# A two-layer encoder in fp32 on one core: V of mixer A computed first, by seven half-sized products per head group, and the merge of each head pair emitted behind the next pair's first projection

## The chip, the cores and the metric

The kernel is one program on one core of a Trainium2 chip. The metric is the device time of one execution in microseconds (us); a kernel's time is the median of its runs. The engines are named as in the profile: PE (matrix products), PEld (its weight loads), DVE (elementwise work), ACT (activations and copies), POOL (a few small operations, and the issue of DMAs that add to what lies in the destination), SP (the issue of all other DMAs).

## The reference

A pre-norm encoder of two layers on x of shape (1, 512, 1024) in fp32. Layer 0 has mixer A, layer 1 mixer B (latent attention), and each mixer is followed by a squared-ReLU MLP of width 4096. The change touches mixer A:

```python
def dilated_mixer(h, w_qkv, q_gain, k_gain, w_o):     # h: [1, 512, 1024]
    qkv = (h @ w_qkv).reshape(B, S, 3, N_GROUPS, A_HEADS, A_HEAD_DIM)   # 3 groups, 8 heads of 128
    for g, (window, dil) in enumerate(((128, 1), (512, 4), (2048, 16))):
        q = rope(rms_norm(qkv[:, :, 0, g], q_gain[g]), S)
        k = rope(rms_norm(qkv[:, :, 1, g], k_gain[g]), S)
        v = qkv[:, :, 2, g]
        o, lse = dilated_group(q, k, v, window, dil)   # banded attention inside each residue class
        ...
    wts = softmax(stack(lses), axis=0)                 # the three groups merged by their denominators
    o = sum(wts[g][..., None] * outs[g])
    return o.reshape(B, S, A_WIDTH) @ w_o
```

So V is, for each of the three groups, one product of a 512x1024 by a 1024x1024 matrix.

## The kernel before, in words

**Products.** Every fp32 operand x is split into hi (a rounded copy, written by ACT, L157 for weights: `whi`) and lo = x - hi (DVE, L158: `wlo`), and a product is three passes, hi·hi, hi·lo and lo·hi, accumulated in a bank of PSUM. `run_block` (L161) takes a matrix in units of two 128-row slices of the weight, loads each unit from SP (`raw`), splits it, and issues its matmuls (L184) for four row tiles r, each with a bank `acc` of its own. The list `groups` says how many units are issued for a row tile before the next row tile comes: with [1, 1, 1, 1] each unit goes through all four tiles, with [4] each tile is finished in one go. `evac` empties a bank when its last unit is through. The activations hT (hi and lo) are the stationary operand, 128x128; the weights move past it, 512 or 384 columns to a matmul.

**Mixer A** runs over four pairs of heads b. A pair has three `qk_block` (L293), one to a group: 96 matmuls of 512 columns, and for each row tile an evacuation with mean squares on ACT (L136), the rotary products on DVE (L308, L311, L315, L316), transposes on PE (L123), and then scores, masks and exponentials. It has two `v_block` (L365), one to a head: 96 matmuls of 384 columns (three groups of 128), copied to `vt`; group 0's part goes to DRAM (`vd`) and comes back in another arrangement as `v0n` and `v0c`. Then `merge` (L376) weights the three groups: small matmuls that move statistics between partitions (`scm`, L386 and L411), some twenty short DVE operations, and six products of the probabilities by the weights (L417). `pv` (L419) transposes the probabilities (L123, copied out at L426) and multiplies by V (L440, L444, into `oT` at L446). In the last pair the order is V of head 0, the three `qk_block`, `merge`, V of head 1, `pv`.

**Behind it** `oT` is split into `oA` (L655, L656), and `project` (L635) multiplies by w_o in two column halves: the first in single units, the second with [4]. The MLP follows; its down projection is made in four quarters, each by seven half-sized products (`wino`, L489; matmuls L580) instead of eight, in the order of the list `ORDER` (L590). A product has its activation operand split at L485 and L486 (`asp`) and its weight at L523 and L524; sums of weights are made by DMAs from POOL that add to what lies in SBUF (L509), sums of activations on DVE (L517).

**What sets the order.** Each engine executes its instructions in one fixed row. The tile framework sets that row at build time: it simulates a timeline and places the instructions of code that is written one after the other among each other. A row of one engine can thus be read before anything runs, and the code alone does not show it.

## Time and profile before

| | |
|---|---|
| median of 3 runs | 1451.21 us (1450.21, 1451.21, 1451.93) |
| profiled execution | 1451.78 us, its span 1449.6 us, mean granted PE clock 0.999 |
| mixer A with its output projection | roughly the first 560 us of the span |
| one middle head pair (256.06 to 379.74 us) | 123.7 us |
| busy | PE 97%, PEld 83%, DVE 61%, ACT 50%, POOL 14% of the span |

Busy times of PE overstate: matmuls overlap, so the mean duration of one (some 340 to 390 ns) is longer than the time from one start to the next. The distance is read from stretches of the chain that ended last in which PE waits for nothing. The clock is 1.00 when the throttle grants full speed. An idle time in brackets in a timeline row is the time that the engine stood before that instruction, with the instruction that released it.

### The profile page before, as it was taken

How to read it: one execution, taken by the hardware profiler on the slowest of the kernel's cores; microseconds unless marked ns; L12 is line 12 of the kernel's file. 1: busy time of each engine (PE TensorE's matmuls, PEld its weight loads, DVE VectorE, ACT ScalarE, POOL GpSimd, SP SyncE). 2: the span in 40 equal slices, each digit the busy share in tenths (PEclk: the TensorE clock that was granted, in tenths of full speed). 3: DMA queues.
4: the chain of work that ended last, by engine and by line, in shares of the span. 5: the costliest groups of instructions: out<-in, count | busy, mean ns of one | idle time of the engine just before them, and what ended most of it. 6: DMA issues, size and time to landing. Idle time of an engine off the chain costs nothing.

```text
span 1449.6 us, 19315 instructions
## 1 busy us (share of the span) xinstructions
PE 1410.4 (97%) x7116; PEld 1196.8 (83%) x7116; DVE 887.1 (61%) x1421; ACT 727.2 (50%) x1590; POOL 198.4 (14%) x197
## 2 busy tenths in 40 slices
PE   7999999999999999999999999899999999999998
PEld 6889889889988878888888877776768988888877
DVE  6765566566537655266475749788755266475647
ACT  5544455355335533453544545777633454544543
POOL 1120120011011101011020222332101011020210
PEclk9999999999999999999999999999999999999999
DMA  7325114321622344749394853310013749394853
GB/s 228 100 57 162 58 49 129 110 63 45 174 92 62 97 140 141 222 112 236 91 233 127 195 136 66 99 30 30 30 44 136 206 111 239 93 223 138 189 116 88
DMA packets 134813, 177.52 MB, mean 122 GB/s; under 512 B 8768, under 2 KB 73536, under 8 KB 134720
## 3 DMA queue, kind: packets, MB, share of 16 engines
q1 hardware_dynamic: 117312, 142.74, 31.1%
q0 software_dynamic: 17408, 33.56, 14.0%
q8 instruction: 56, 0.92, 0.2%
q14 instruction: 37, 0.30, 0.1%
HBM read 172.07 MB, written 4.19 MB: 122 GB/s over the span
## 4 chain that ended last, share of the span: by engine, by line
PE 89%; ACT 4%; DVE 3%; DMA 2%; issue 1%; POOL 1%; SPq 0%; DVEq 0%; ACTq 0%; POOLq 0%
PE acc L184 58%; PE sc L580 10%; PE tp L580 7%; PE tp L123 4%; PE acc L859 1%; PE acc L835 1%; PE sc L753 1%; PE sco L444 1%; PE sco L440 1%; PE sc L351 1%; PE sc L835 1%; ACT whi L157 1%; ACT junkb L136 1%; DVE wlo L158 1%; PE tp L859 0%
## 5 line engine op out<-in xcount | busy, mean ns | idle before, releaser
L184 PE MATMUL acc<-whi,hT 128*128 128x512 f32 (+2 forms) x1600 | 486.3, 379 | 5.6 <-DVE t L311 2.2
L158 DVE TENSOR_TENSOR wlo<-raw,whi 128x1024 fp32r<-128x1024 f32 (+3 forms) x170 | 195.7, 1156 | 230.5 <-ACT whi L157 229.5
L184 PEld LDWEIGHTS acc<-whi,hT 128*128 128x128 f32 x1600 | 296.2, 189 | 47.3 <-issue 2.9
L184 PE MATMUL acc<-hT_f,whi 128*128 128x512 f32 (+1 forms) x1152 | 319.4, 366 | 1.9 <-DVE resid L641 1.2
L157 ACT ACTIVATE whi<-raw 128x1024 fp32r<-128x1024 f32 (+3 forms) x170 | 170.0, 1005 | 269.0 <-PE acc L184 177.4
L184 PE MATMUL acc<-wlo,hT 128*128 128x512 f32 (+2 forms) x800 | 300.2, 375 | 0.2 <-DVE wlo L158 0.2
L184 PEld LDWEIGHTS acc<-hT_f,whi 128*128 128x128 f32 x1152 | 208.4, 189 | 37.8 <-DVE resid L641 1.6
L524 DVE TENSOR_TENSOR wlo<-wqs,whi 128x1024 fp32r<-128x1024 f32 x112 | 137.3, 1227 | 113.6 <-ACT whi L523 113.5
L184 PE MATMUL acc<-hT_f,wlo 128*128 128x512 f32 (+1 forms) x576 | 205.1, 365 | 0.0
L523 ACT ACTIVATE whi<-wqs 128x1024 fp32r<-128x1024 f32 x112 | 118.6, 1060 | 167.6 <-PE acc L184 66.2
L184 PEld LDWEIGHTS acc<-wlo,hT 128*128 128x128 f32 x800 | 151.2, 189 | 20.5 <-DVE wlo L158 1.1
L580 PE MATMUL sc<-whi,asp 128*128 128x512 f32 x512 | 165.1, 390 | 0.8 <-ACT asp L485 0.8
L509 POOL DMA_DIRECT2D wqs<-in_ffn_w_dram x64 | 77.6, 1350 | 528.4 <-DVE wlo L524 339.9
L184 PEld LDWEIGHTS acc<-hT_f,wlo 128*128 128x128 f32 x576 | 108.6, 189 | 17.5
L131 POOL TENSOR_TENSOR qrs<-rs_v,nhalf 128x4 f32<-128x4 f32 x48 | 61.5, 1290 | 408.3 <-DVE rs_v L128 393.8
L580 PE MATMUL tp<-whi,asp 128*128 128x512 f32 x352 | 112.2, 390 | 2.6 <-DVE asp L486 2.6
L580 PEld LDWEIGHTS sc<-whi,asp 128*128 128x128 f32 x512 | 96.1, 188 | 21.6 <-ACT asp L485 1.6
L580 PE MATMUL sc<-wlo,asp 128*128 128x512 f32 x256 | 99.6, 389 | 0.0
L580 PEld LDWEIGHTS tp<-whi,asp 128*128 128x128 f32 x352 | 65.9, 188 | 17.2 <-DVE asp L486 3.5
L580 PE MATMUL tp<-wlo,asp 128*128 128x512 f32 x176 | 68.5, 389 | 0.0
L136 ACT ACTIVATE junk<-acc 128x128 f32<-128x128 f32 x192 | 53.1, 277 | 18.9 <-PE acc L184 13.8
L554 DVE TENSOR_TENSOR resid<-resid,sc 128x512 f32<-128x512 f32 x64 | 43.0, 682 | 24.4 <-PE sc L580 24.4
(190 smaller groups left out, 1796.3 us busy)
## 6 DMA issues: line engine op xcount, KB each, us to landing
wqs<-in_ffn_w_dram SPq DMA_DIRECT2D x80, 512.0 KB, 5.1
raw<-in_ffn_w_dram SPq DMA_DIRECT2D x64, 512.0 KB, 4.4
wqs<-in_ffn_w_dram POOLq DMA_DIRECT2D x64, 512.0 KB, 7.2
raw<-in_a_w_qkv_dram SPq DMA_DIRECT2D x96, 256.0 KB, 3.4
raw<-in_a_w_qkv_dram SPq DMA_DIRECT2D x64, 192.0 KB, 2.8
raw<-in_a_w_o_dram SPq DMA_DIRECT2D x8, 512.0 KB, 4.0
raw<-in_b_w_o_dram SPq DMA_DIRECT2D x8, 512.0 KB, 3.7
xt<-in_x_dram SPq DMA_DIRECT2D x8, 256.0 KB, 5.7
```

The lines of the kernel that those rows point to most:

```text
L123: PE.transpose(o, i, ident)
L131: G.tensor_tensor(out, v[:, :n], nhalf[:, :n], op=ALU.pow)
L136: A.activation(junk, x, AF.Square, scale=1.0 / math.sqrt(dim), accum_out=out)
L157: A.activation(hi[:, :nk, :n], raw[:, :nk, :n], AF.Copy)
L158: V.tensor_tensor(lo[:, :nk, :n], raw[:, :nk, :n], hi[:, :nk, :n].bitcast(F32), op=ALU.subtract)
L184: PE.matmul(accs[o][:, oc], lhsT=lt, rhs=rt, start=(kt == 0 and p_i == 0 and hv == 0), stop=(kt == total - 1 and p_i == 2), skip_group_che ...
L509: nc.gpsimd.dma_start(t, src, accum_op=ALU.add)
L523: A.activation(hi, x, AF.Copy)
L524: V.tensor_tensor(lo, x, hi.bitcast(F32), op=ALU.subtract)
L554: V.tensor_tensor(sl, sl, banks[t], op=op)
L580: PE.matmul(bk[t], lhsT=lt, rhs=rt[:, j], start=(first and k == 0 and i_ == 0), stop=(k == 3 and i_ == 2), skip_group_check=True)
L835: PE.matmul(sc, lhsT=lt, rhs=rt, start=(i == 0), stop=(i == 4))
```

## The change

1. **V phase.** `v_phase` computes V of all heads before the pairs. For each group the 512x1024 by 1024x1024 product is cut into 2x2 blocks and made by seven products of half size in each dimension, 24 matmuls of 512 columns each, instead of eight. The sums of activations that the products need (`Ssp`, from copies `h32` and `stg` of the transposed rows) are made once, on DVE. Of the sums of weights one is added on DVE (`sum1`, `bT`), one on DVE (`b3`), and two are made by adding DMAs from POOL (`add_block`, 2 of 512 KB each). Banks are emptied by `put` into `vo`, and V goes to DRAM (`vall`). The Q and K projection of pair 0, group 0 is made inside this phase, by code of its own, ahead of the products. The v_block of before, their loads and their copies are gone.
2. **Pairs.** `v_load` reads a pair's V back from DRAM. The Q and K projections use groups [2, 2] instead of [1, 1, 1, 1]. `scores` and the projection of the next group alternate, and `finish` (merge and pv) of pair b is emitted behind the first projection of pair b+1.
3. **Last pair.** `oA` is split for heads 0 to 5, and the first three of the four units of the output projection's first column half (they need only heads 0 to 5) are emitted ahead of `finish`; the fourth unit follows the last `pv`.
4. **Last down projection** of each MLP: `ORDER_LAST` moves product 2 ahead of products 5 and 3.

The diff, cut to its core:

```diff
-    def run_block(units, groups, n, mm, evac, outs=NT, name=None, halves=1):
+    def block_groups(units, groups, n, mm, outs=NT, halves=1):
...
-                        evac(o, accs[o])
+                        yield o, accs[o]
             kt0 = nkt
+            if gi < len(groups) - 1:
+                yield None
...
+    def qk_proj(b, g, qkT, homes, junk):
+        run_block(qk_units(b, g), [2, 2], 512, act_stationary(hT, 512),
+                  lambda r, acc: qk_evac(g, qkT, r, acc, homes, junk)())
...
+        def add_block(t, g, ki, ni):
+            for u in range(2):
+                nc.gpsimd.dma_start(t[:, 2 * u:2 * u + 2], wblk(g, ki, ni, u), accum_op=ALU.add)
...
+        def sum1(g, u):
+            us = slice(2 * u, 2 * u + 2)
+            V.tensor_tensor(bT[g][:, us], b11[g][:, us], b12[g][:, us], op=ALU.add)
...
+        def piece(g, ba, bd, parts):
+            put(g, 0, 0, "set", ba, False)
+            put(g, 0, 0, "add", bd, True)
+            bb = new_banks("b")
+            both(5, bT[g], bb, True, parts)
+            put(g, 1, 1, "set", bb, False)
+            add_block(bT[g], g, 1, 1)
+            both(3, b22[g], bb, False, parts)
+            put(g, 0, 1, "set", bb, False)
+            b3 = vp.tile([P, 4, 512], F32, tag="h32", name=nm("b3"))
+            for u in range(2):
+                us = slice(2 * u, 2 * u + 2)
+                V.tensor_tensor(b3[:, us], b12[g][:, us], b22[g][:, us], op=ALU.add)
+            both(6, bT[g], ba, False, parts)
+            put(g, 0, 1, "sub", ba, True)
+            add_block(bT[g], g, 1, 0)
+            both(7, b3, ba, False, parts)
+            put(g, 1, 1, "sub", ba, True)
+            both(4, bT[g], ba, False, parts)
+            put(g, 1, 0, "set", ba, True)
...
+        for g in range(1, NG):
+            fetch(g)
+            parts = {}
+            ba, bd = new_banks("a"), new_banks("d")
+            both(1, b11[g], ba, True, parts)
+            both(2, b21[g], bd, True, parts)
+            for u in range(2):
+                sum1(g, u)
+            piece(g, ba, bd, parts)
...
-            if last:
-                vs = [v_all(0)]
-                qk_all()
-                merge(stats, Pt, True)
-                vs.append(v_all(1))
-                oA = new_hT()
-            else:
-                qk_all()
-                vs = [v_all(0), v_all(1)]
-                merge(stats, Pt, False)
-            for h in range(2):
-                pv(b, h, Pt, *vs[h])
+            vs = v_load(b)
+            for g in range(NG):
+                scores(b, g, qkT, Pt, stats)
+                if g + 1 < NG:
+                    qkT = project_in(b, g + 1)
+            if b + 1 < HA // 2:
+                qkT = project_in(b + 1, 0)
+                finish(b, Pt, stats, vs)
+        oA = new_hT()
...
+        for h in range(HA - 2):
+            split_o(h)
+        first_cols = block_groups(w_units(a_w_o[0], 0, 512), [3, 1], 512, act_stationary(oA, 512))
+        next(first_cols)
+        finish(HA // 2 - 1, Pt, stats, vs)
+        for h in (HA - 2, HA - 1):
+            split_o(h)
...
-        for p, chain, first, (i, n, op) in ORDER:
+        for p, chain, first, (i, n, op) in ORDER if done is None else ORDER_LAST:
...
+    ORDER_LAST = [ORDER[0], ORDER[4]] + ORDER[1:4] + ORDER[5:]
```

Three places show what this does to the rows of the engines.

DVE's row at the start of mixer A, before: `cosg` and `sing` are the rotary tables, `hT` the lo part of the last row tile, `t` the rotary products of the first two banks.

```order
L289 TENSOR_TENSOR cosg_104<-ca,gqk 128x4x128
L291 TENSOR_TENSOR sing_107<-ca,gqk 128x4x128
L289 TENSOR_TENSOR cosg_104<-ca,gqk 128x4x128
L291 TENSOR_TENSOR sing_107<-ca,gqk 128x4x128
L221 TENSOR_TENSOR hT_91<-tp_212,hT_91 128x4x128
L221 TENSOR_TENSOR hT_91<-tp_219,hT_91 128x4x128
L308 TENSOR_TENSOR t_59_296<-acc_243,cosg_104 128x512
L311 TENSOR_TENSOR t_60_297<-acc_243,sing_107 128x4x64 x2
```

The same stretch of DVE's row now, from the lo part of the last row tile to the first split of a V weight (`bT` is a sum of weight blocks, `Ssp` and `stg` belong to the sums of activations, `wlo_408` is the lo part of the first V weight):

```order
L408 TENSOR_TENSOR stg_241<-stg_241,h_109 128x512
L362 TENSOR_TENSOR hT_91<-tp_257,hT_91 128x4x128
L362 TENSOR_TENSOR hT_91<-tp_262,hT_91 128x4x128
L272 TENSOR_TENSOR t_51_382<-acc_141,cosg_103 128x512
L272 TENSOR_TENSOR t_55_399<-acc_142,cosg_103 128x512
L275 TENSOR_TENSOR t_51_382<-acc_141,sing_104 128x4x64 x2
L275 TENSOR_TENSOR t_55_399<-acc_142,sing_104 128x4x64 x2
L448 TENSOR_TENSOR bT_158<-b_11_146,b_13_152 128x1024 x2
L128 TENSOR_SCALAR rs_v_522<-qss_513 128x4
L384 TENSOR_TENSOR Ssp_115<-stg_241,Ssp_115 128x4x128
L372 TENSOR_TENSOR stg_271<-h_109,stg_271 128x512
L422 TENSOR_TENSOR wlo_408<-b_11_146,whi_407 128x1024
```

The four table operations still stand right ahead of these rows; sums of weights and of activations have come in between the rotary products and the next split of a weight.

PE's row around the last pair's merge, before: `acc_4717` is the last bank of V of head 1, `sc` the last group's scores, `acc_4987` and on the banks of the output projection's first column half, `scm` the merge's small matmuls.

```order
L184 MATMUL acc_4717<-wlo_4815,hT_91 128x384
L184 MATMUL acc_4717<-whi_4814,hT_91 128x384
L351 MATMUL sc_4654<-qkT_4433 128x128
L351 MATMUL sc_4666<-qkT_4433 128x128
L351 MATMUL sc_4654<-qkT_4433 128x128
L351 MATMUL sc_4666<-qkT_4433 128x128
L184 MATMUL acc_4987<-whi_4993,hT_4858 128x512
L184 MATMUL acc_4987<-wlo_4994,hT_4858 128x512
L184 MATMUL acc_4988<-whi_4993,hT_4858 128x512
L184 MATMUL acc_4988<-wlo_4994,hT_4858 128x512
```

Behind these come, before, the merge's first small matmuls, some 60 matmuls of the output projection, and its second small matmuls. The same place in PE's row now (`acc_4589` is the last of the output projection's four banks, with the third of its units, `whi_4604`, at the end):

```order
L183 MATMUL acc_4589<-wlo_4599,hT_4573 128x512
L183 MATMUL acc_4589<-whi_4598,hT_4573 128x512
L592 MATMUL sc_4549<-qkT_4328 128x128
L592 MATMUL sc_4561<-qkT_4328 128x128
L183 MATMUL acc_4589<-whi_4604,hT_4573 128x512
L183 MATMUL acc_4589<-wlo_4605,hT_4573 128x512
L183 MATMUL acc_4589<-whi_4604,hT_4573 128x512 x2
L183 MATMUL acc_4589<-wlo_4605,hT_4573 128x512
L183 MATMUL acc_4589<-whi_4604,hT_4573 128x512
L630 MATMUL scm_4683<-ca,xsel_4680 128x4 x4
L655 MATMUL scm_4704<-ca,xsel_4680 128x4 x2
L123 MATMUL tp_4714<-ck,P_4022 128x128 x4
```

The output projection's 72 matmuls stand ahead of and among the last scores, six of them behind; between the merge's two small steps and the transposes stands nothing else.

DVE's row at the start of the last down projection, before (`wlo` are weight splits, `S` sums of activations, `asp` the lo parts of activations, `resid` the results):

```order
L524 TENSOR_TENSOR wlo_12129<-wqs_10046,whi_12128 128x1024
L524 TENSOR_TENSOR wlo_12145<-wqs_10046,whi_12144 128x1024
L517 TENSOR_TENSOR S_12121<-a_2046_11516 128x1024
L517 TENSOR_TENSOR S_12162<-S_12121,a_2046_11516 128x1024
L524 TENSOR_TENSOR wlo_12169<-wqs_10046,whi_12168 128x1024
L554 TENSOR_TENSOR resid<-resid,sc_12085 128x512
L486 TENSOR_TENSOR asp_12123<-S_12121,asp_12123 128x4x256
```

And now:

```order
L784 TENSOR_TENSOR wlo_11878<-wqs_9795,whi_11877 128x1024
L784 TENSOR_TENSOR wlo_11894<-wqs_9795,whi_11893 128x1024
L777 TENSOR_TENSOR S_11913<-a_2007_11265 128x1024
L746 TENSOR_TENSOR asp_11872<-a_2007_11265,asp_11872 128x4x256
L777 TENSOR_TENSOR S_11954<-S_11913,a_2007_11265 128x1024
L814 TENSOR_TENSOR resid<-resid,sc_11834 128x512
L784 TENSOR_TENSOR wlo_11921<-wqs_9795,whi_11920 128x1024
L746 TENSOR_TENSOR asp_11915<-S_11913,asp_11915 128x4x256
```

The second product's operand no longer is a sum; the sum's lo part (`asp_11915`) stands one product later in PE's use.

## The prediction

> **What bounds the kernel now.** The page's head and its summary of the chain that ended last come first.

> ```profile
> span 1449.6 us, 19315 instructions
> PE 1410.4 (97%) x7116; PEld 1196.8 (83%) x7116; DVE 887.1 (61%) x1421; ACT 727.2 (50%) x1590; POOL 198.4 (14%) x197
> PE 89%; ACT 4%; DVE 3%; DMA 2%; issue 1%; POOL 1%; SPq 0%; DVEq 0%; ACTq 0%; POOLq 0%
> ```

> PE is the bound, and the other engines release it seldom. So matmuls removed count in full wherever PE stays fed, and the price of one must be a distance from start to start. I take it from two stretches of the chain in which PE waits for nothing, the first of 512 columns, the second (the two v_block of a pair) of 384; the three rows behind show a middle pair's merge.

> ```profile
> 29.36 9.80 PE acc L184 x43
> 362.57 17.17 PE acc L184 x99
> ...
> 256.06 0.79 PE scm L386 x8
> 256.85 8.08 PE acc L184 x35
> 264.93 0.34 PE scm L411 x4
> ```

> 9.80/43 = 0.2279 us for 512 columns, 17.17/99 = 0.1734 us for 384. In the merge, 35 matmuls of other work already stand between its two steps. The table by windows (us, then busy time of PE, PEld, DVE, ACT, POOL with instruction counts, PE clock, DMA share, GB/s) tells the same of a whole middle pair, and of the 47 us in it in which DVE has most to do.

> ```profile
> 256.00:380.00 124.00, 123.97 (x706) 111.74 (x704) 74.33 (x143) 59.68 (x190) 14.75 (x12) 1.00 0.29 84
> 315.00:362.00 47.00, 46.97 (x260) 42.24 (x259) 32.55 (x68) 26.65 (x96) 10.38 (x8) 1.00 0.15 43
> ```

> PE is busy all of both. Where PE does wait is in the list of its waits (us, times, longest), and its largest stall inside mixer A in a timeline and three windows:

> ```profile
> PE tp L580 <- DVE asp L486: 2.6, 2, 1.5
> PE acc L184 <- DVE t L311: 2.2, 1, 2.2
> PE sc L580 <- ACT asp L485: 0.8, 2, 0.4
> ...
> 91.04 0.39 PE L184 MATMUL acc<-whi,hT 128*128 128x512 f32 x1
> 93.67 0.41 PE L184 MATMUL acc<-whi,hT 128*128 128x384 f32 x1 [2.24 <-DVE t L311]
> ...
> 94.00:96.00 2.00, 2.00 (x11) 2.00 (x10) 2.00 (x5) 1.34 (x5) 0.00 (x0) 0.76 0.71 205
> 96.00:98.00 2.00, 2.00 (x8) 2.00 (x7) 2.00 (x5) 0.13 (x2) 0.93 (x1) 0.50 0.45 126
> 98.00:100.00 2.00, 2.00 (x11) 2.00 (x11) 2.00 (x5) 0.00 (x0) 2.00 (x2) 0.89 0.50 133
> ```

> A v_block waited there 93.67 - 91.04 - 0.23 = 2.4 us for a bank of the qk_block ahead, and the clock then fell: 2 us x (0.24 + 0.50 + 0.11) = 1.7 us lost.

> **The change part by part.** *V's products.* 8 heads x 96 = 768 matmuls of 384 go, 3 x 7 x 24 = 504 of 512 come: -768 x 0.1734 + 504 x 0.2279 = -133.2 + 114.9 = -18.3. [...]

> *The stall at 91 us* goes with the v_block: -4.1.

> *The start.* Each of the four row tiles gets another copy or two on ACT before the next can be transposed. A weight's hi copy and one such copy in the chain, and DVE's own prices (starts apart, from rows with more than one instruction):

> ```profile
> 9.38 1.06 ACT whi L157
> 10.43 0.49 ACT hT L220
> ...
> 508.01 1.89 DVE L656 TENSOR_TENSOR hT<-oT,hT 128x512 fp32r<-128x512 f32 x3
> 498.91 2.36 DVE L158 TENSOR_TENSOR wlo<-raw,whi 128x1024 fp32r<-128x1024 f32 x2 [2.22 <-ACT whi L157]
> 486.05 0.74 DVE L311 TENSOR_TENSOR t<-acc,sing 128x256 f32<-128x256 f32 x2
> ```

> Three of 128x512 end in 1.89 and one takes 0.68, so one each 0.605; likewise 1.14 for 128x1024 and 0.36 for 128x256. The start costs one copy, +0.5, the others run beside the matmuls of the row tile ahead.

> *V phase, group 0.* From the last row tile's transposes to product 1's first use of `wlo_408`, PE has 36 matmuls (30 of Q and K, 6 that need only hi parts): 8.2 us. DVE has, in its row, four tables (2.42), a sum (0.61), two lo parts (1.21), rotary products for two banks (2 x 0.605 + 4 x 0.36 = 2.65), `bT` (2.28), two short steps of the sums (1.21), one small (0.1) and the split (1.14): 11.6. PE waits 3.4. Bounds: 0 if the tables are done before the transposes land; 11.6 if nothing covers.

> *Group 0 to 1.* Between the split for product 7 and that for the next group's product 1 DVE has four splits (4.56), two emptied banks (1.21), `b3` and `sum1` (2.28 each) and the split (1.14): 11.5, against 38 matmuls, 8.7: +2.7 (0 to 11.5). Groups 1 and 2 have no evacuation of Q and K beside them, and 168 matmuls (38.3 us) to 14 splits, 4 additions and 10 emptied banks or so (26.6): 0.

> *Adding DMAs.* 12 from POOL of 512 KB; the same kind is there in the MLP:

> ```profile
> L509 POOL DMA_DIRECT2D wqs<-in_ffn_w_dram x64 | 77.6, 1350 | 528.4 <-DVE wlo L524 339.9
> wqs<-in_ffn_w_dram POOLq DMA_DIRECT2D x64, 512.0 KB, 7.2
> ```

> 1.35 to issue, 7.2 to land, 2.2 for the split (1.06 and 1.14): 10.75. Splits stand a product ahead in DVE's row, so two products, 48 matmuls or 10.9 us, cover it: 0, but with 0.2 to spare. Bounds 0 and 6 x 10.75 = 64 without any cover. SP's loads of whole blocks and the stores of V come to about 8 MB in 38 us, 210 GB/s; around 95 us the windows above show 205.

> *Pairs.* A pair loses 192 matmuls of 384: 123.7 - 33.3 = 90.4 us of PE. DVE loses 8 splits of 128x768:

> ```profile
> L158 DVE TENSOR_TENSOR wlo<-raw,whi 128x768 fp32r<-128x768 f32 x11 | 10.5, 956 | 19.6 <-ACT whi L157 19.4
> ```

> 74.3 - 8 x 0.956 = 66.7 us, 74% of 90.4; in the 47 us window, with as much density as the pair now has throughout, it was 32.55, 69%, and PE never stood. So 0, with [2, 2] too: the last 48 matmuls leave 12 (2.7 us) from one bank's end to the next, and its rotary products take 1.3. Bounds: -2 (the short waits between scores go) and +8 (a wait of 0.5 at each of sixteen later row tiles). The moved merges of pairs 0 to 2 gain nothing, since 8.08 us of work covered them: 0.

> *The last pair.* Before, on PE, DVE and ACT:

> ```profile
> 482.60 0.39 PE L184 MATMUL acc<-whi,hT 128*128 128x512 f32 x1
> 484.13 0.41 PE L184 MATMUL acc<-whi,hT 128*128 128x384 f32 x1 [1.15 <-ACT junk L136]
> ...
> 503.54 1.05 PE L351 MATMUL sc<-qkT 128*128 128x128 f32 x8
> 504.81 0.50 PE L184 MATMUL acc<-whi,hT 128*128 128x512 f32 x1 [0.21 <-ACT hT L655]
> 521.99 0.50 PE L411 MATMUL scm<-ca,xsel 128*128 128x4 f32 x4
> 525.75 0.66 PE L123 MATMUL tp<-ck,P 128*128 128x128 f32 x4 [2.09 <-DVE pT L426]
> 540.00 0.50 PE L184 MATMUL acc<-whi,hT 128*128 128x512 f32 x1 [0.98 <-ACT hT L655]
> ...
> 504.41 1.29 DVE L356 TENSOR_TENSOR P<-sc,ca 128x512 f32<-128x512 f32 x2 [1.01 <-PE sc L351]
> 515.34 0.18 DVE L398 TENSOR_TENSOR mw<-me,stat 128x24 f32<-128x24 f32 x1
> 516.82 2.49 DVE L417 TENSOR_TENSOR P<-P,me 128x512 f32<-128x512 f32 x4
> ...
> 510.01 0.40 ACT L362 ACTIVATE P<-P,stat 128x128 f32<-128x128 f32 x1 [1.71 <-DVE stat L360]
> 512.73 0.39 ACT L362 ACTIVATE P<-P,stat 128x128 f32<-128x128 f32 x1
> ```

> From the last Q and K matmul to scores, V of head 1 covered the rotary work (96 x 0.1734 = 16.6); from scores to the merge's second step, 17.4 us, some 60 matmuls of the output projection covered the softmax. PE's idle time from there to the end of the first column half was 1.15 + 0.21 + 2.09 + 0.98 = 4.4 in these rows, about 5.9 of 59.6 us with the shorter ones. Now V is not there, and 66 of the 72 matmuls (15.0 us) are spent on the first gap. Between scores and transposes stand 6 of them (1.4 us) against two masks and two maxima (4 x 0.605 = 2.4), eight exponentials (3.1, from 510.01 to 513.1), the merge's dozen small steps (0.18 each, 2.2), two crossings of PE (1) and two of the products L417 ahead of the first transposes (1.2): about 10, so PE stands 8.6 in one piece. With the rotary work's end (about 2), `pv`'s two copies (2.6) and the split of heads 6 and 7 (1.0), idle is 14.2: +8.3. Lower bound -3, if the exponentials run beside the masks and the small steps beside the last matmuls; upper +17.4 - 1.4 = 16 (nothing gets shorter). A clock loss comes with it: the 2.24 us stall cost 1.7; two windows like that, at 8.6 us, say +2.5 (0 to 7). [...]

> *Last down projections.* The wait for `asp` at product 5, in both layers, is 2.6 + 0.8 = 3.4 in all, and product 2's operand needs no sum: -2.0 (0 to -3.4; the rest is the split itself, which is only one operation shorter).

> *Sum:* -18.3 - 4.1 + 0.5 + 3.4 + 2.7 + 8.3 + 2.5 - 2.0 = -7.0. 1451.8 - 7.0 = 1444.8 for the profiled execution, which lies 0.6 above the median: 1444.

> **The rivals.** *The added chains are hidden.* If the scheduler's row lets DVE start tables and sums before the transposes land, and the last merge costs no more than before: -18.3 - 4.1 + 0.5 - 2.0 = -23.9, 1427; with half of the last merge's loss 1433. For it speaks DVE's 61%, against it the rows, which put four tables ahead of the last lo parts.

> *The adding DMAs become the wait.* 0.2 us of slack is less than the scatter of landing times; if each of six sums comes 1 us late, +6: 1450, no change that can be told. For it: each is issued only once the split of the old sum is through. Against it: the MLP has 64 of them and its PE list shows no wait for one.

> *Slower: the stall at 91 us comes back in each pair.* It arose where a new block needed the bank that DVE's rotary products still held. Q and K projections now follow each other with no V between; when DVE's work in a pair passes PE's 90.4 us (it needs 24 us more than the 66.7, or a backlog of 3 us at a pair's start from `finish`), every pair pays 2.24 + 1.7 = 3.9, 4 x 3.9 = 15.6: 1460. Against it: the 47 us window.

> *The change does not do what it says:* PE's row holds 504 matmuls for V and no v_block, so this has no share; for the moved merges it is already in the sum as 0.

> **How the numbers follow.** Forecast 1444, 0.47; chains hidden, 1427 to 1436, 0.20; DMAs, 1450, 0.21; slower, 1460, 0.12. A measurement of this kernel tells about 0.2% from no change, that is below 1448.3 or above 1454.1. Faster: 0.47 + 0.20 = 0.67; same 0.21; slower 0.12. The range reaches up to 1454, which leaves out the last case, and down to 1433, which leaves out some 0.08 of the hidden chains.

> **What would show it.** V phase: 504 matmuls at 0.228; a wait for `wlo` or the emptied bank near 35 us and again some 40 us later. Pairs of about 90 us with PE at 100%. A PE gap of 8 us or more between the last scores and the transposes, with a clock of 0.5 behind it. No `asp` wait at product 5. Wrong it is if that gap is under 4 us (then 1436), if PE waits for a sum from POOL's DMAs in each group, or if pairs take over 95 us.

## The result, and the profile after

The change makes the kernel slower: a median of 1459.29 us (1455.49 to 1461.88, 10 runs) against 1451.96 us (1449.91 to 1454.19, 10 runs), a ratio of 1.0051 with a 95% interval of 1.004 to 1.0062. Forecast was 1444. The profiled execution of the changed kernel took 1455.49 us and is the fastest of the ten; 3.8 us lie between it and the median, and they belong to the explanation.

The head of the page and its summary of the chain that ended last:

```profile
span 1453.7 us, 18783 instructions
PE 1398.6 (96%) x6852; PEld 1162.4 (80%) x6852; DVE 941.1 (65%) x1477; ACT 749.6 (52%) x1606; POOL 221.1 (15%) x209
PE 84%; DVE 6%; ACT 4%; DMA 2%; issue 2%; POOL 1%; SPq 0%; DVEq 0%; ACTq 0%; POOLq 0%
```

PE has less to do and a smaller share of the chain, DVE twice the share that it had. The pairs are as forecast. Two starts of a pair's merge in the chain, and a window of 125 us inside the pairs (columns as before: busy of PE, PEld, DVE, ACT, POOL, then clock, DMA share, GB/s):

```profile
332.56 0.79 PE scm L630 x8
422.82 0.79 PE scm L630 x8
...
200.00:325.00 125.00, 125.00 (x687) 107.07 (x686) 92.29 (x182) 69.33 (x241) 20.02 (x17) 1.00 0.28 86
```

A pair takes 90.26 us (forecast 90.4); in that window DVE is busy 74% of the time and PE never stands. The loss is in three other places. Of PE's waits over the whole span (us, times, longest), these rows bear on them:

```profile
PE scm L655 <- DVE xsel L650: 8.0, 1, 8.0
PE sc L840 <- ACT whi L783: 4.5, 1, 4.5
PE acc L433 <- DVE vo L461: 2.8, 4, 1.3
...
PE acc L433 <- DVE wlo L422: 2.6, 2, 1.6
...
PE tp L433 <- ACT qkT L290: 1.2, 1, 1.2
...
PE acc L397 <- DVE hT L362: 1.0, 1, 1.0
...
PE acc L397 <- DVE wlo L422: 1.0, 1, 1.0
```

**The last merge.** PE's timeline there, and the clock in windows behind it:

```profile
510.24 1.05 PE L630 MATMUL scm<-ca,xsel 128*128 128x4 f32 x8
519.33 0.99 PE L655 MATMUL scm<-ca,xsel 128*128 128x4 f32 x4 [8.04 <-DVE xsel L650]
...
511.00:515.00 4.00, 0.29 (x3) 0.20 (x2) 3.93 (x11) 1.01 (x4) 0.00 (x0) 0.84 0.74 251
515.00:519.00 4.00, 0.00 (x0) 0.00 (x0) 1.02 (x7) 2.79 (x15) 0.00 (x0) 0.50 0.45 138
519.00:521.00 2.00, 1.67 (x8) 1.70 (x9) 2.00 (x5) 0.00 (x0) 0.00 (x0) 0.50 0.00 0
521.00:523.00 2.00, 1.60 (x8) 1.20 (x6) 2.00 (x5) 0.00 (x0) 0.00 (x0) 0.50 0.00 0
523.00:525.00 2.00, 1.41 (x6) 0.74 (x5) 2.00 (x3) 0.13 (x1) 0.00 (x0) 0.50 0.00 0
525.00:527.00 2.00, 1.61 (x8) 1.61 (x9) 0.34 (x1) 0.92 (x2) 0.00 (x0) 0.50 0.00 0
```

One bare stretch of 8.04 us, and the clock is at half from within it until 527 us. The two PE rows show it as well: four tiny matmuls take 0.99 us behind the gap, eight took 1.05 ahead of it.

**Layer 0's last down projection.** POOL's timeline, and the ACT and PE rows that wait for it:

```profile
864.15 0.52 POOL L956 TENSOR_TENSOR cgB<-ck,gr 128x128 f32<-128x128 f32 x1 [26.08 <-DMA gr<-in_b_q_gain_dram]
872.64 1.71 POOL L958 TENSOR_SCALAR sgB<-sgB 128x256 f32<-128x256 f32 x1
874.31 2.50 POOL L769 DMA_DIRECT2D wqs<-in_ffn_w_dram  x2
...
880.72 1.06 ACT L783 ACTIVATE whi<-wqs 128x1024 fp32r<-128x1024 f32 x1 [5.04 <-DMA wqs<-in_ffn_w_dram]
...
881.83 0.81 PE L840 MATMUL sc<-whi,asp 128*128 128x512 f32 x2 [4.45 <-ACT whi L783]
```

POOL stood idle for 26 us until a small load released it, then worked through nine table operations of mixer B (864.15 to 874.3), and only then issued the adding DMAs that product 6 needs. The tables are first read at 925 us.

**The V phase.** The five last rows of the waits, 8.6 us in all: PE waits for DVE (weight splits, emptied banks) or for what stands behind DVE's work.

An account of where the time went: from one PE start to the next I took what goes beyond the usual distance of that shape (the median, 0.227 us for 512 columns; a shorter distance counts as negative), and summed it by stretch. It holds waits and half clock together; the stretches that are left out hold less than 0.5 us each.

| stretch, us | before | changed kernel | second profile of it (e1) | forecast of the difference |
|---|---|---|---|---|
| 0 to 125 (most of the V phase; before, the stall at 91) | 9.0 | 14.3 | 14.7 | +2.5 |
| 125 to 475 (pairs) | 2.6 | 3.0 | 3.7 | 0 |
| 475 to 600 (last merge, output projection) | 8.7 | 22.0 | 25.1 | +10.8 |
| 850 to 900 (layer 0's last down projection) | 3.7 | 6.7 | 6.4 | -1.0 |
| 900 to 1125 (mixer B) | 36.1 | 36.4 | 36.5 | 0 |
| 1400 to 1450 (layer 1's last down projection) | 2.0 | 1.5 | 1.5 | -1.0 |

The sums are 62.1, 83.9 and 87.9. Less the 18.3 us of V's matmuls the difference is +3.5 and +7.5, and the spans differ by +4.1 and +7.8.

### The profile page after: what moved, and what is told of

It reads as the page before. It is cut to its first block, busy times and chain, and to the rows that moved or that the text cites. A ratio compares the mean times of both kernels' runs of the same rounds, so it can differ in the third digit from the quotient of the medians.

```text
span 1453.7 us, 18783 instructions
## 1 busy us (share of the span) xinstructions
PE 1398.6 (96%) x6852; PEld 1162.4 (80%) x6852; DVE 941.1 (65%) x1477; ACT 749.6 (52%) x1606; POOL 221.1 (15%) x209
## 3 DMA queue, kind: packets, MB, share of 16 engines
q0 software_dynamic: 20672, 39.85, 16.6%
## 4 chain that ended last, share of the span: by engine, by line
PE 84%; DVE 6%; ACT 4%; DMA 2%; issue 2%; POOL 1%; SPq 0%; DVEq 0%; ACTq 0%; POOLq 0%
PE acc L183 47%; PE sc L840 11%; PE tp L840 8%; PE tp L123 4%; PE acc L433 3%; PE tp L433 2%; PE acc L1124 1%; PE sc L1018 1%; PE acc L1100 1%; PE sco L685 1%; PE sco L689 1%; PE sc L592 1%; DVE wlo L156 1%; PE sc L433 1%; PE sc L1100 1%
## 5 line engine op out<-in xcount | busy, mean ns | idle before, releaser
L183 PE MATMUL acc<-whi,hT 128*128 128x512 f32 (+1 forms) x1024 | 329.0, 395 | 1.9 <-ACT hT L731 1.0
L156 DVE TENSOR_TENSOR wlo<-raw,whi 128x1024 fp32r<-128x1024 f32 (+3 forms) x134 | 160.3, 1201 | 161.0 <-ACT whi L155 160.2
L183 PEld LDWEIGHTS acc<-whi,hT 128*128 128x128 f32 x1024 | 190.5, 188 | 39.4 <-ACT hT L731 1.7
L155 ACT ACTIVATE whi<-raw 128x1024 fp32r<-128x1024 f32 (+3 forms) x134 | 138.4, 1040 | 153.7 <-PE acc L183 67.3
L183 PE MATMUL acc<-wlo,hT 128*128 128x512 f32 (+1 forms) x512 | 201.5, 395 | 0.0
L769 POOL DMA_DIRECT2D wqs<-in_ffn_w_dram x64 | 77.6, 1341 | 516.9 <-DVE wlo L784 323.2
L183 PEld LDWEIGHTS acc<-hT_f,wlo 128*128 128x128 f32 x576 | 109.3, 190 | 17.5
L131 POOL TENSOR_TENSOR qrs<-rs_v,nhalf 128x4 f32<-128x4 f32 x48 | 69.9, 1459 | 316.6 <-DVE rs_v L128 278.5
L183 PEld LDWEIGHTS acc<-wlo,hT 128*128 128x128 f32 x512 | 96.4, 188 | 17.3 <-issue 0.2
L136 ACT ACTIVATE junk<-acc 128x128 f32<-128x128 f32 x176 | 48.5, 275 | 48.9 <-PE acc L183 44.1
L290 ACT ACTIVATE qkT<-tp 128x512 f32<-128x512 f32 x48 | 36.0, 764 | 47.4 <-PE tp L123 47.3
## 6 DMA issues: line engine op xcount, KB each, us to landing
wqs<-in_ffn_w_dram SPq DMA_DIRECT2D x80, 512.0 KB, 5.0
raw<-in_ffn_w_dram SPq DMA_DIRECT2D x64, 512.0 KB, 4.3
wqs<-in_ffn_w_dram POOLq DMA_DIRECT2D x64, 512.0 KB, 7.2
b<-in_a_w_qkv_dram SPq DMA_DIRECT2D x24, 512.0 KB, 6.6
bT<-in_a_w_qkv_dram POOLq DMA_DIRECT2D x12, 512.0 KB, 6.2
vt<-vall SPq DMA_DIRECT2D x8, 512.0 KB, 4.4
```

The lines of the kernel that those rows point to most:

```text
L131: G.tensor_tensor(out, v[:, :n], nhalf[:, :n], op=ALU.pow)
L136: A.activation(junk, x, AF.Square, scale=1.0 / math.sqrt(dim), accum_out=out)
L155: A.activation(hi[:, :nk, :n], raw[:, :nk, :n], AF.Copy)
L156: V.tensor_tensor(lo[:, :nk, :n], raw[:, :nk, :n], hi[:, :nk, :n].bitcast(F32), op=ALU.subtract)
L183: PE.matmul(accs[o][:, oc], lhsT=lt, rhs=rt, start=(kt == 0 and p_i == 0 and hv == 0), stop=(kt == total - 1 and p_i == 2), skip_group_che ...
L290: A.activation(dst, tv, AF.Copy)
```

## The experiments

Theory A: the loss is the bare last merge with its half clock, the adding DMA that waits behind table operations on POOL, and DVE at the start. Its rivals are named in the expectations. Each ratio is against the kernel before, in runs on the same chip.

### The changed kernel again (e1_again)

> The changed kernel once more, unaltered, as the measure for the other runs on this chip and for a second profile. Theory A (the loss sits at three places: the last pair's merge without cover, with a half clock behind it; the wait for an adding DMA in layer 0's last down projection; DVE in the V phase): 1.004 to 1.006 times before, the same PE gap of 8 us behind the merge's first small step, and a mean clock near 0.99. If its runs again scatter by some 5 us, a profile with another time than 1455.5 shows where: by theory A in the length of the half-clock stretch. Rival B (the loss is spread over the pairs): PE's idle time between 125 and 475 us is over 5 us.

1458.65 us, 1.0046 (1.0032 to 1.0061). Its profile took 1457.4 us of span, 3.7 more than the first. The gap is the same 8.19 us from start to start, and what differs is the clock. The windows of the new profile, and last the one of the first profile at the same place:

```profile
525.00:527.00 2.00, 1.44 (x8) 1.04 (x7) 1.21 (x2) 0.60 (x1) 0.00 (x0) 0.50 0.00 0
527.00:530.00 3.00, 3.00 (x16) 3.00 (x15) 0.00 (x0) 0.60 (x1) 0.00 (x0) 0.50 0.00 0
570.00:575.00 5.00, 3.17 (x16) 2.82 (x15) 4.34 (x7) 1.75 (x3) 0.55 (x1) 0.74 1.03 356
...
570.00:575.00 5.00, 5.00 (x43) 5.00 (x44) 3.14 (x5) 2.14 (x3) 0.55 (x1) 1.00 1.03 375
```

Half clock lasts to 530 us and beyond, and a short stall near 570 us brings it a second time, which in the first profile it did not. Of the 4.0 us by which the account grows, 3.1 lie in this stretch. Rival B is out: 3.7 us in the pairs.

Finer windows show in what the two profiles differ there, two of the second profile and last one of the first:

```profile
569.00:572.40 3.40, 1.32 (x8) 0.67 (x6) 3.40 (x5) 2.11 (x4) 0.00 (x0) 1.00 0.79 236
572.40:575.80 3.40, 3.40 (x16) 3.40 (x17) 2.45 (x4) 0.71 (x2) 0.55 (x1) 0.50 1.04 373
...
568.30:571.70 3.40, 2.05 (x16) 1.85 (x17) 2.74 (x5) 1.65 (x3) 0.55 (x1) 1.00 1.01 383
```

Half clock comes in steps of 3.4 us in these traces: one step here, four steps (513.7 to 527.4 us) in the first profile, five (514.4 to 531.4) at the merge in the second. Three single steps of the first profile begin at 882.36, 940.38 and 1117.88 us, 108, 125 and 177 times 3.413 us behind 513.72; the one at 572.4 us in the second lies 12 times that behind 531.4. In the 3.4 us ahead of the step at 572.4 us PE was busy for 1.32 us, 39% of the time; in the kernel before it was 1.33 of 3.40 us ahead of the half clock at 95 us, and ahead of the first profile's three single steps 0.54, 1.40 and 1.48 of 3.41. In the first profile the same three waits near 570 us (0.25, 0.48 and 1.35 us) are parted by the steps, counted on from 513.7 us: PE is busy for 2.05 us of the later one, and the clock stays at 1.00. So it is not the length of a stall alone, but how much of one step the waits fill, that goes with the half clock here, and the two profiles of one kernel have their steps at different places. No run was made to move a stall against the steps.

### The kernel before with a bare last merge (e2_before_uncovered)

```diff
-                vs = [v_all(0)]
+                vs = [v_all(0), v_all(1)]
                 qk_all()
                 merge(stats, Pt, True)
-                vs.append(v_all(1))
```

> The kernel before with one thing changed: in the last pair V of head 1 is projected ahead of the three Q and K blocks instead of behind the merge. No V phase, no half-sized products, the same instructions. Theory A: the last merge is bare, PE stands about 8 us in one piece, the clock falls to half behind it, and the kernel is 9 to 14 us slower than before (1461 to 1466). Rival C (the gap costs little since before has idle time of its own there): 0 to 4 us slower.

1464.51 us against 1451.01: +13.5, 1.0092 (1.0078 to 1.0105). The same instructions in another order cost as much as theory A says, without any of the rest of the change. PE's wait at the merge in this kernel:

```profile
PE scm L411 <- DVE xsel L406: 5.8, 1, 5.8
```

The wait itself is 5.8 us here, not the 8 in one piece that were expected; the other 7.7 are left for shorter waits around it and for the clock (a mean of 0.991 in this profile, 0.999 in that of the kernel before). Rival C is out.

### The kernel before with the new order of products (e3_before_new_order)

The edit is the last hunk of the change alone.

> The kernel before with only the new order of products in the last down projections. Theory A: in POOL's row the nine table operations of mixer B come to stand ahead of all adding DMAs of layer 0's last down projection; PE waits 3 to 5 us for one of them there, so 1 to 4 us slower than before (the waits for the split sums that go are worth 2 to 3). Rival D (the wait in the changed kernel comes from the V phase's or the tail's shift of the whole row, not from the order): 2 us faster, as forecast.

1453.93 us, +2.9, 1.0019 (1.0009 to 1.0029): slower, where this step of the forecast had -2.0. The wait is the one of the changed kernel, in a kernel with no V phase:

```profile
PE sc L580 <- ACT whi L523: 4.2, 1, 4.2
```

POOL's row explains it. In the kernel before, one DMA more stands ahead of the tables, and one ahead of the last of them; its POOL timeline there:

```profile
857.21 1.20 POOL L509 DMA_DIRECT2D wqs<-in_ffn_w_dram  x1 [20.56 <-DVE wlo L524]
864.01 1.08 POOL L691 TENSOR_TENSOR cgB<-ck,gr 128x128 f32<-128x128 f32 x1 [5.60 <-DMA gr<-in_b_q_gain_dram]
...
872.89 1.19 POOL L509 DMA_DIRECT2D wqs<-in_ffn_w_dram  x1
873.68 1.55 POOL L693 TENSOR_SCALAR sgB<-sgB 128x256 f32<-128x256 f32 x1
```

With the new order the row is:

```order
L509 DMA wqs_5335<-in_ffn_w_dram 128x2x512 x28
L693 TENSOR_TENSOR cgB<-ck,gr 128x4x32
L694 TENSOR_TENSOR sgB<-ck,gr 128x4x32
L693 TENSOR_TENSOR cgB<-ck,gr 128x4x32
L694 TENSOR_TENSOR sgB<-ck,gr 128x4x32
L693 TENSOR_TENSOR cgB<-ck,gr 128x4x32
L694 TENSOR_TENSOR sgB<-ck,gr 128x4x32
L693 TENSOR_TENSOR cgB<-ck,gr 128x4x32
L694 TENSOR_TENSOR sgB<-ck,gr 128x4x32
L695 TENSOR_SCALAR sgB<-sgB 128x8x32
L509 DMA wqs_5335<-in_ffn_w_dram 128x2x512 x4
```

Before, 29 DMAs stood ahead of these nine. Product 5 is later in the new order, so its sum is free later, and the row was set with the tables in between.

### Mixer B's tables on DVE (e4_tables_on_dve)

```diff
-                    G.tensor_tensor(cgB[:, :, t, hf * 32:hf * 32 + 32], cosB, gb, op=ALU.mult)
-                    G.tensor_tensor(sgB[:, :, t, hf * 32:hf * 32 + 32], sinB, gb, op=ALU.mult)
-            G.tensor_scalar(sgB[:, :, :, 32:64], sgB[:, :, :, 32:64], -1.0, None, op0=ALU.mult)
+                    V.tensor_tensor(cgB[:, :, t, hf * 32:hf * 32 + 32], cosB, gb, op=ALU.mult)
+                    V.tensor_tensor(sgB[:, :, t, hf * 32:hf * 32 + 32], sinB, gb, op=ALU.mult)
+            V.tensor_scalar(sgB[:, :, :, 32:64], sgB[:, :, :, 32:64], -1.0, None, op0=ALU.mult)
```

> The changed kernel with mixer B's nine table operations issued on DVE instead of POOL. Theory A: POOL issues the adding DMAs as soon as the old sum is split, the PE wait of 4.5 us in layer 0's last down projection goes, with 1 to 2 us of half clock: 3 to 6 us faster than the changed kernel, 1453 to 1456. Rival E (the adding DMA is late through its own chain of splits): no change.

1455.74 us, 2.9 less than the changed kernel, at the edge of what was expected: 1.0034 (1.0022 to 1.0047). The wait for `whi` is gone, but smaller ones came: the tables now stand in DVE's row from 869.4 to 871.0 us, ahead of a sum for which ACT then waits 1.97 us. In PE's list:

```profile
PE sc L840 <- DVE resid L814: 1.6, 1, 1.6
PE sc L840 <- ACT asp L745: 1.1, 1, 1.1
```

### More cover ahead of the merge, without and with the old order (e5_more_cover, e6_more_cover_old_order)

```diff
-        first_cols = block_groups(w_units(a_w_o[0], 0, 512), [3, 1], 512, act_stationary(oA, 512))
-        next(first_cols)
+        mm_o = act_stationary(oA, 512)
+        run_block(w_units(a_w_o[0], 0, 512)[:3], [3], 512, mm_o,
+                  lambda r, acc: A.activation(oT[:, r], acc, AF.Copy))
+        second = block_groups(w_units(a_w_o[0], 512, 512), [3, 1], 512, mm_o, outs=2)
+        next(second)
...
-        for p, chain, first, (i, n, op) in ORDER if done is None else ORDER_LAST:
+        for p, chain, first, (i, n, op) in ORDER_LAST if done is not None and tag == 7 else ORDER:
```

The second hunk is in e6 alone.

> The changed kernel with more work to lay under the last merge: the first three units of the output projection's first column half go to SBUF (ACT copies into the halves of oT that are already split), and three units of the second half are multiplied for two of the four row tiles ahead of the merge (36 more matmuls, 8.2 us); the rest follows behind pv. Theory A: the 8 us gap and the half clock behind it go, 10 to 14 us faster than the changed kernel, 1445 to 1449. Rival C (the merge's chain only moves, and pv's chain or the end of the output projection pays instead): 0 to 4 us faster.

> As the kernel with more cover, and layer 0's last down projection in the old order of products (layer 1's stays new). Theory A: another 2 to 4 us, 1442 to 1446, with no wait over 2 us in that projection. Rival D (the order is not the cause): the same as with more cover alone.

e5: 1452.25 us, 1.0009 (1.0001 to 1.0018), 6.4 less than the changed kernel; between the two theories. e6: 1451.71 us, 1.0003 (0.9994 to 1.0012), only 0.5 less again, which the runs do not tell apart; by the time alone this is rival D's outcome. The traces part the two: e5's wait of 4.4 us for `whi` in layer 0's last down projection is gone in e6, and the account of 850 to 900 us falls from 7.1 to 3.9, but that of 900 to 1125 us rises from 33.2 to 36.9. Why mixer B was quicker in e5's profile is open. PE's timeline of e5 says why the cover is worth half:

```profile
519.19 0.73 PE L630 MATMUL scm<-ca,xsel 128*128 128x4 f32 x6
524.56 0.78 PE L655 MATMUL scm<-ca,xsel 128*128 128x4 f32 x3 [4.65 <-DVE xsel L650]
```

All 36 matmuls stand ahead of the end of the first crossing; the softmax is covered now, the dozen small steps between the crossings are not, and 4.65 us are still enough to bring the half clock (0.50 from 523.4 to 533.6 us).

### The first sum by DMA (e7_sum_by_dma)

```diff
-            bT[g] = vp.tile([P, 4, 512], F32, tag="wq", name=nm("bT"), bufs=5)
+            bT[g] = block(g, 0, 0, "bT")
+            add_block(bT[g], g, 0, 1)
...
-            V.tensor_tensor(bT[g][:, us], b11[g][:, us], b12[g][:, us], op=ALU.add)
```

> The changed kernel with the first sum of weights of each group (bT) made by a load and an adding DMA instead of on DVE: 2.28 us of DVE less and 1 MB of DMA more in each group. Theory A (DVE is the bound where PE waits in the V phase): PE's idle time up to 125 us falls from 14.5 to 8 to 11, 3 to 6 us faster. Rival G (the DMA queue is as full as DVE there): new waits for bT, no faster or up to 6 us slower.

1459.42 us, 1.0057 (1.0043 to 1.007): no gain, so rival G holds for the sum of both effects. By stretches the two theories share it. From 25 to 50 us PE's loss falls from 3.3 to 1.4 us: there DVE was the bound. Behind that ACT, which makes the hi parts, waits for `bT` to land: 17.9 us in eight pieces, against 4.0 in two in the changed kernel, and one of PE's waits for an emptied bank grows in group 1:

```profile
PE acc L433 <- DVE vo L461: 3.3, 3, 2.6
```

### Single units in the projections (e8_single_units)

```diff
-        run_block(qk_units(b, g), [2, 2], 512, act_stationary(hT, 512),
+        run_block(qk_units(b, g), [1, 1, 1, 1], 512, act_stationary(hT, 512),
```

> The changed kernel with the Q and K projections in groups [1, 1, 1, 1] as before, instead of [2, 2]. Theory A and the forecast (DVE's work fits into the pairs with either): within 2 us of the changed kernel. Rival H (the grouping is what keeps the stall that was at 91 us from coming back between projections): PE waits for L272 or L275 of 1 to 2.5 us in each pair, 5 to 16 us slower.

1459.09 us, 1.0054 (1.0041 to 1.0067), the changed kernel's time. The grouping does not decide it, and the stall at 91 us does not come back in each pair with single units either: PE waits nowhere longer than 0.3 us for the rotary products, once 1.67 us for another short step of DVE (at 192 us) and once 1.32 us in a merge (at 336 us). The rival that the prediction gave for "slower" did not happen.

### Cover between the crossings, and a pace that fell (e9_cover_between, e10_between_order_sum, e11_between_aligned, e13_shift_32_bytes, e16_shift_128_bytes)

To hold the second half's matmuls back, the copies that free their banks are multiplied by a one that depends on the merge's first result:

```diff
+            one = st.tile([P, 1], F32, tag="one", name="one", bufs=1)
+            V.tensor_scalar(one, m[:, 0, 0, 0:1], 0.0, 1.0, op0=ALU.mult, op1=ALU.add)
+            for r, acc in firsts:
+                A.activation(oT[:, r], acc, AF.Copy, scale=one)
+            next(second)
```

> The changed kernel with the same 36 extra matmuls as the kernel with more cover, but held back until the merge's first crossing of PE is through (the copies that free their banks are scaled by a one that is worked out from the merge's first result). Theory A, sharpened by the runs so far (cover ahead of the first crossing is spent there, and the 4.8 us from the first to the second crossing stay bare): the 36 matmuls now lie between the two crossings, PE waits under 1.5 us there, the half clock behind them goes, 9 to 13 us faster than the changed kernel, 1446 to 1450. Rival C (the wait moves to the transposes and pv, since DVE has the same chain to run): as with cover ahead, 1451 to 1453.

> As the kernel with the cover between the crossings, with layer 0's last down projection in the old order of products, and the sum bT of group 0 alone (not of groups 1 and 2) by a load and an adding DMA. Theory A: all three places mended, each by its own size, 3 (order, as measured on the kernel before) and 1 to 2 (DVE at the start) on top: 1441 to 1446, faster than both kernels. Rival D (the gains don't add, other stalls bring the half clock instead): 1447 to 1451.

1476.75 and 1469.85 us, 1.0182 (1.0163 to 1.02) and 1.0133 (1.0115 to 1.0151): far off both theories. Two causes show in e9's trace. The copies stood behind the exponentials in ACT's row, so PE waited 7.01 us all the same:

```profile
520.26 2.38 ACT L745 ACTIVATE oT<-acc,one 128x512 f32<-128x512 f32 x4
...
520.98 0.79 PE L183 MATMUL acc<-whi,hT 128*128 128x512 f32 x1 [7.01 <-ACT oT L745]
```

And every matmul of the MLPs was slower. The same 179 matmuls of layer 0's MLP in the chain of e1 and of e9:

```profile
682.96 40.57 PE acc L183 x179
```

```profile
686.65 41.77 PE acc L183 x179
```

40.57/179 = 0.2266 us and 41.77/179 = 0.2334, at a granted clock of 1.00 in both (every window of 5 us from 680 to 725). The tile `one`, 4 bytes of a partition, takes 32, and everything allocated behind it moved by 32 bytes in the build's allocation: `hT_f` from byte 135872 of each partition to 135904, the MLP's activations and their split parts likewise; the weights' hi and lo and mixer A's `hT` stayed. e10 has the same addresses, and it too is slow (1469.85 us). Three runs on that; the second and third leave the changed kernel as it is but for an unused tile and the one DVE operation that fills it.

> As the kernel with the cover between the crossings, but the extra small tile takes 64 bytes of a partition instead of 4. Theory K (the last two runs were slow because the extra tile moved every tile allocated behind it by 32 bytes: in their profiles each matmul of the MLP takes 0.233 us from start to start instead of 0.227, and hT_f, the MLP's activations and their split parts begin at a multiple of 32 and no longer of 64 bytes): the pace is back at 0.227, and about 22 us of the loss with it; the tail then is that of the last profile, so 1453 to 1458, since the copies that free the banks stood behind the exponentials there and PE still waited 7 us. Rival L (the pace fell for the extra dependencies or from the chip): 1470 or more.

> The changed kernel with nothing but one unused tile of 32 bytes of a partition among the small tiles, written once, so that all tiles allocated behind them lie 32 bytes further. Every instruction of PE and its order are the same. Theory K: 1478 to 1482, with 0.233 us instead of 0.227 from matmul to matmul in the MLP. Rival L: 1459, as the changed kernel.

> The changed kernel with an unused tile of 128 bytes of a partition among the small tiles, all else unaltered. Theory K in the narrower form (the pace hangs on where operands lie modulo 128 bytes: 64 in the changed kernel for the activations and the weights, 96 with the tile of 32 bytes, 0 with that of 64): 1459, pace 0.227. Rival M (any shift slows, or the sum of addresses counts): 1465 to 1477.

e13: 1476.14 us, 1.0174 (1.0157 to 1.0191), 17.5 us slower than the changed kernel through 32 unused bytes. e16, 128 bytes: 1475.04, 1.0162 (1.0148 to 1.0176). e11, 64 bytes: 1471.39, 1.0135 (1.0119 to 1.015). The chain of e13 and of e16:

```profile
688.25 41.77 PE acc L185 x179
```

```profile
687.05 41.60 PE acc L185 x179
```

Theory K holds in its first half: the shift alone makes the pace. Its rule does not: neither the address modulo 64 nor modulo 128 bytes tells which shift is slow, since 64 and 128 bytes are slow too. What fits all these runs is how far apart a matmul's two operands lie in the partition. In the fast kernels it is a multiple of 512 bytes for each of these matmuls (the tiles are a multiple of 1024 apart: `hT_f` at 135872, `whi` at 63168). With the activations 32 bytes off that, the mean distance of starts is 0.2333 us; 128 bytes off, 0.2324 and 0.2325 in the two projections; 64 bytes off (e12), 0.2290 in the first projection of the MLP, where the activations move past the weights, and 0.2333 in the down projection, where they are the stationary operand. V's products on the sums `Ssp`, which had moved too, slow down with them, and those on `hT` do not: in 5 us of full PE its weight loads take 4.04 and 4.00 us in e9 and 4.13 in the changed kernel where the products are on `Ssp` (100 to 110 us), 4.14 in both on `hT` (90 to 95 us). No run was made to test this, and other distances were not tried.

### All three places mended (e12_third_tile_between, e14_third_between_same_place, e15_second_between_same_place)

e12 holds back one row tile of three; e14 is e12 with `one` in a tile that exists already, so that nothing moves; e15 holds back the second of two row tiles. All three have layer 0's old order of products and group 0's `bT` by DMA.

```diff
+            one = rqs[0][:, 0, 0:1]
...
             for r, acc in firsts:
-                A.activation(oT[:, r], acc, AF.Copy, scale=one)
+                if r >= 1:
+                    A.activation(oT[:, r], acc, AF.Copy, scale=one)
+                else:
+                    A.activation(oT[:, r], acc, AF.Copy)
```

(this is e15; in e12 and e14 the condition is r == 2, and three row tiles are taken.)

> The changed kernel with three of four row tiles of the second column half as cover, two ahead of the first crossing and only the third (18 matmuls, 4.1 us) held back until the first crossing is through, an extra tile of 64 bytes, layer 0's last down projection in the old order, and bT of group 0 by DMA. Theory A: the 8 us of bare chain are covered but for 1 to 2 us, and the three places together give 1444 to 1448, faster than both kernels. Rival D (what is saved in one place is lost to the half clock of the next stall): 1449 to 1453.

> As the kernel with the third tile between the crossings, but the small operand of the held-back copy lies in a tile that is there already, so no tile moves. Theory K: matmul pace 0.227 again (the last profile had 0.229 and 0.233 in the MLPs, which over some 3000 matmuls is 12 to 14 us): 1444 to 1448. The end of the output projection may keep some 4 us, since the norms of three row tiles now end together (the last profile: 8.6 us of PE's idle time from 550 to 575 us, against 4.1).

> The same, but with two instead of three row tiles of the second column half as cover, one ahead of the first crossing and one behind it, so that two row tiles are left for the end. Theory A: the bare chain is covered but for 1 to 3 us and the end of the output projection is as in the changed kernel: 1442 to 1447, the fastest so far. Rival D: 1448 to 1452.

e12: 1459.66 us, 1.006 (1.0047 to 1.0073), with the slow pace again (its 64 bytes; 40.99 us for 179 matmuls in the same row, and 5.60 us instead of 5.44 for 24 of the down projection). e14: 1448.95 us, 0.9983 (0.9974 to 0.9992). e15: 1448.85 us, 0.9984 (0.9975 to 0.9993). Both beat the kernel before by about 2.6 us and the changed one by 10, and both miss what was expected of them, e14 by 1, e15 by 2, which puts e15 into rival D's range. What is left shows in their waits, e14's first, e15's PE timeline second:

```profile
PE tp L123 <- DVE hT_f L227: 4.1, 3, 1.8
PE sco L692 <- DVE pT L678: 2.9, 2, 1.7
PE acc L183 <- ACT hT_f L226: 2.3, 2, 2.1
```

```profile
514.91 0.50 PE L183 MATMUL acc<-whi,hT 128*128 128x512 f32 x1 [3.11 <-ACT oT L751]
```

In e14 the gap at the merge is gone, and the wait has moved to the norms at the end of the output projection (the account has 8.2 us from 550 to 575, against 2.8 in the changed kernel). In e15 the copies still stand behind the exponentials, for 3.1 us. Work under the merge is work taken from under something else: by the account, 475 to 600 us holds 21.5 us in e14 and 20.9 in e15, against 25.1 in e1 and 8.7 before, so only a quarter of the loss there came back at best; the rest of the gain is the start and the order (e15: 0 to 125 us 11.7, 850 to 900 us 3.3). Holding the cover back bought nothing that shows: with all of it ahead of the first crossing that stretch holds 20.2 us in e5 and 21.8 in e6, and what e14 and e15 gain over e6 lies in the first 125 us (14.8 us in e6).

## Why the prediction was wrong, step by step

**V's products, right.** 504 matmuls of 512 columns at 0.227 us, forecast 0.228: the half-sized products do save the 18 us.

**The pairs, right.** 90.26 us against 90.4, DVE at 74%, no wait. The grouping does not decide the time (e8); the moved merges were set to 0, and no run tried them alone.

**Start and V phase, mis-sized: +6.6 forecast, 8.6 us of waits measured**, by the account +5.3 instead of +2.5 with the old stall taken off. The two waits that were worked out from DVE's rows came, a little smaller: 2.6 us at 35.5 and 43.3 us for 3.4, and 2.3 us at 80.0 and 84.5 us for 2.7 (the prediction's own 11.5 less 8.7 is 2.8). What was set to 0 was not: at 55.7 us product 5 waits 1.2 us for ACT's copies of the transposed Q and K, and at product 7 of group 1 there are waits of 0.4 and 0.9 us for a bank that DVE empties behind a split and `b3`.

**The last merge, the right mechanism, too small: +10.8 forecast, +13.5 (e2), +13.3 and +16.4 in the two profiles.** The gap was forecast at 8.6 us and measured 8.04. PE's listed waits from 475 to 602 us add up to 5.9 us before and to 15.2 in both profiles, +9.3 where +8.3 was forecast. The part that was too small is the clock behind the gap, +2.5, against the 4.0 and 7.1 us that the account holds beyond these waits: half clock lasts from about 514 to 527 us in one profile and to 531 in the other, where a stall of 1.4 us near 570 us brings it again. The windows from 570 us have 0.74 in one profile and 1.00 in the other at the same stall. The 2.5 was an estimate, two falls like the one at 91 us with its 1.7; no run shows that a gap of 8 us costs two of them. What the traces show is one step of half clock behind that stall, and four and five from within the gap on: PE worked 1.67 + 1.60 + 1.41 + 1.61 = 6.3 us in the first profile's windows from 519 to 527 us, by their clock of 0.50 an estimated 3.1 lost. Nor did PE have to stand through a whole step: it was busy for 39% of the one ahead of the second half clock (e1). In the second profile half clock lasts one step longer, behind the same waits (0.40, 0.43 and 0.56 us): in its last step but one PE is busy for 2.82 of 3.40 us, in the last step of the first profile for 2.84. What decides between the two is open.

**The last down projections, wrong in sign: -2.0 forecast, +2.9 measured (e3).** This is the step whose mechanism failed. It was read from DVE's row and PE's list of waits alone. The waits for `asp` at product 5 did go, as forecast, but the new order moves the adding DMA for product 6 to a later place in POOL's row, behind nine operations for which nobody waits, which in turn wait for a small load; PE then waits 4.45 us for it. The term for the adding DMAs had been set to 0 for the V phase alone, and the change of order was not asked about POOL: POOL's row before and after shows it, and could have been read beforehand.

**The step to the median, wrong: -0.6 forecast, +3.8 measured.** The first profile is the fastest of ten runs, which is luck. Over these ten the mean granted clock goes with the time, from 0.991 in the fastest to 0.988 in the slowest (1461.88 us). The second profile is of a run at the median (1459.23 us), and 3.1 of the 4.0 us that its account holds more lie behind the last merge. So most of this step is the clock behind the gap once more.

Taken from the second profile, the account differs from the forecast by 5.6 us in the last merge, 4.2 in the two last down projections, 3.2 up to 125 us, 1.1 in the pairs and 0.4 in mixer B: 14.5 of the 14.8 us by which its span is off, all one way. The failed step alone does not make the miss; the clock behind the gap is as large. Of the terms with bounds only the order's was left (0 to -3.4); the upper ends of the others stood in the text, but the range was made as if they could not come together. "Slower" had 0.12, on a mechanism that did not happen.

## What to carry to other kernels

A block of work that is moved to the front takes its cover with it: before counting what it saves, list what it hid where it stood, and what hides that now. Cover that is spent ahead of the first of several dependent steps leaves the later ones bare (4.65 us in e5), and cover that is held back for them was taken from somewhere else (e14). Read the row of every queue that issues something for a moved step, the idle one above all: an engine at 15% busy made PE wait 4.5 us because nine operations without urgency stood in front of two DMAs. And after any edit that adds a tile, compare the pace of matmuls that the edit does not touch, before reading the time as its effect.

## What the runs showed of the hardware that was not expected

An unused tile of 32 bytes of a partition made the kernel 17.5 us slower: matmuls whose activations had moved took 0.2334 us instead of 0.2266 (41.77/179 in e13, 40.57/179 in e1), those of mixer A on `hT`, which had not moved, kept theirs (3.41/15 = 0.2273 from 528.17 to 531.58 us of e9). With 64 bytes it was 0.2290 (40.99/179, e12) in the first projection of the MLP and 0.2333 (5.60/24) in the down projection, with 128 bytes 0.2324 (41.60/179). The clock was 1.00 over those of e9 and e12; the mean of a whole profile was 0.990 with 32 unused bytes and 0.988 with 128, against 0.991 and 0.989 in the changed kernel's two.
